# Buffer lifetimes that count transfers, and a re-ordered feed-forward schedule, in a one-core diffusion step

## Chip, cores and metric

The kernel runs on one core of one Trainium2 chip. The metric is the device time of one launch in microseconds (us), here the median of three runs. TensorE is called PE, VectorE DVE, ScalarE ACT, GpSimd POOL and SyncE SP, as in the profile.

## What is computed

One inference step of a hybrid diffusion backbone with two layers over 128 prompt tokens and 1024 sample tokens, model width 1024. Layer 0 mixes tokens with a gated long convolution (Hyena), layer 1 with differential attention; each is followed by a gated ConvFFN of hidden width 2816. Cut to what matters here, each layer is:

```python
hp = modulate(rmsnorm(xp, norm_w[i, 0]), mp[0], mp[1])       # xs in the same way, with ms
yp = hyena_mixer(hp, ...) if i % 2 == 0 else diff_attention(...) @ at_w_out[j]
xp = xp + mp[2] * rmsnorm(yp, norm_w[i, 1])
hp = modulate(rmsnorm(xp, norm_w[i, 2]), mp[3], mp[4])
xp = xp + mp[5] * rmsnorm(conv_ffn(hp, *ff), norm_w[i, 3])

def conv_ffn(h, w_up, w_dw, b_dw, w_down):
    u = dwconv3(h @ w_up, w_dw, b_dw)
    g, val = jnp.split(u, 2, axis=-1)
    return (jax.nn.silu(g) * val) @ w_down
```

The modulations `mp`, `ms` are `silu(cond) @ w_ada + b_ada`, six vectors of 1024 for each layer and each of the two conditions. All of it is float32.

## The kernel before

**Arithmetic.** A float32 operand is split into two parts of PE's format, `hi` and `lo` (`split`, L207), and a product is three matmuls: hi by hi, hi by lo, lo by hi. The split is made in one of two ways: ACT writes `hi` (L208) and DVE writes `lo = src - hi` (L213); or, with `dma=True`, ACT writes `hi` (L208) and `-hi` (L210), and POOL issues a transfer that adds the source onto it (L211, `lo<-s`, `lo<-wr` in the profile).

**Order of work.** The program is a generator-driven list of steps, written out by hand. Each engine runs its instructions in the order in which the program emits them, so an instruction that waits holds all behind it on its engine. The program runs first in a dry mode (`Dry`, L39): it counts operations on a clock and notes for every on-chip buffer when it was made and last used. `place` (L82) then gives each buffer an address in one arena, larger ones first, wanting first a distance of 1000 operations between the last use of what lay there and the new use, then less, down to 0; it tries fillings of the arena of 100%, 98% and so on down. A buffer that takes the place of another waits for the last instructions that used it. A buffer that a transfer reads or writes counts as free from the operation after the one that issued the transfer.

**The ConvFFN** (`ffn`, L634; it runs twice) takes nine tiles of 128 tokens in three columns of three tiles. Phase 1 loops over 22 groups `g` of 128 hidden channels for the first column: `up` for the gate and the value (24 matmuls each, lines L657 to L659), `conv` and `gate_val` on ACT and DVE, and `down0(g - 1)` (L680) into six of the eight PSUM banks, which stay pinned. Two banks rotate among everything else. After `down0` a queue of generators is advanced (`advance`, L603): first the norms of the tiles of the other columns, `prenorm_pair` (L481), whose two halves each transpose four blocks into a bank (L500) and evict it with four ACT instructions (L503, `hc`); then `combine` (L529), which builds the seven operands of a Strassen-like product. Phase 2 takes columns two and three together, in 22 steps `j` of seven products (`product`, L727, matmuls at L736, 12 each). Helpers lie along the products by the table `ALONG`: `total` sums weights on DVE (L709, tile `s`), `both` splits by the transfer (tile `lo`), `evac` takes results out of PSUM (L740 on DVE, L745 on ACT), `side` and `middle` convolve. The helpers of the steps before the first product (t from -19 to -1) are called at the ends of groups 19 to 21 in phase 1. After the first two products `down0(21)` and `tail(0)` follow: the post-norm (`postnorm`, L584) of the first column, for which `tail` loads three tiles `x` (L579).

**Modulations of the next layer** come from the generator `extra` over `ada_rows` (L346): each step issues on SP a load of 512 KB (`adaw`), and runs two 1024-wide DVE instructions (L372) on the tile loaded a step earlier. It is stepped once for each of nine tiles in the output projection ahead of the ConvFFN (the loop at L1983), after `down0` in groups below 13 of phase 1, and in odd steps of phase 2. One of its steps announces by its value (`busy`) that PE work follows in the next one; the queue isn't advanced in between. On the way it calls `ab_from` (L380), which loads a small vector (`abw`) and uses it at once on DVE.

The few lines that set the order around the change are in phase 1 of `main`:

```python
if g > 0:
    down0(g - 1)
if g > 1 and not busy:
    advance(queue, 2 if g < 9 else 1)
busy = next(extra, None) if g < 13 else None
split_w(g, 2)
if g == NJ - 1:
    advance(queue, -1)
for t in range(6 * (g - NJ), 6 * (g - NJ) + 6):
    if t >= -19:
        along(t)
```

## Time and profile before

| what | value |
|---|---|
| median of three runs | 3182.41 us (3173.52 to 3183.02) |
| profiled execution, its own time | 3175.89 us |
| span of the profile, first to last instruction | 3174.1 us |
| busy share of the span: PE, DVE, ACT, POOL | 97%, 67%, 54%, 20% |
| mean granted TensorE clock | 0.986 |
| DMA, mean over the span | 164 GB/s |

The span is the time from the first to the last instruction, and 1.8 us of the profiled execution lie around it. The waits of an engine are its idle times, each put down to the last instruction or transfer that released it. The granted clock is 1.00 at 2.4 GHz and 0.50 at 1.2 GHz; a window over a stretch gives its mean.

### The profile page before, as it was taken

The numbers are of one execution on the slowest core, as the hardware profiler recorded it, in microseconds if no ns is written. First come the engines' busy times: TensorE is split into PE (matmuls) and PEld (weight loads), VectorE is DVE, ScalarE is ACT, GpSimd is POOL, SyncE is SP. The second block draws the span as 40 slices with busy tenths as digits, with TensorE's granted clock in tenths as the row PEclk, the third lists the DMA queues.
The fourth block names the chain that finished last, engine by engine and source line by source line (L and its number), as shares of the span: only waits on it lengthen the run. The fifth ranks groups of instructions, "written<-read, shape, count | busy, mean of one in ns | idle before, by whom it ended". The sixth has DMA issues, their size and how long they took to land.

```text
span 3174.1 us, 46733 instructions
## 1 busy us (share of the span) xinstructions
PE 3063.5 (97%) x17332; PEld 2839.3 (89%) x17332; DVE 2136.7 (67%) x3057; ACT 1720.0 (54%) x3185; POOL 619.3 (20%) x1010
## 2 busy tenths in 40 slices
PE   8999999899998899999999999999999998999998
PEld 5999998678997899988899999999888998999987
DVE  5678887765775777775654447789465666767743
ACT  5444445444544566654533338899535445666632
POOL 3111111230001222301133422223220002222100
PEclk9999999999999999999999999999999999999999
DMA  6354455853435788786464464353453346888753
GB/s 250 91 138 124 110 135 145 220 201 138 164 115 163 171 197 196 161 303 237 174 197 154 136 190 112 98 140 104 147 204 128 108 139 156 189 181 189 228 203 123
DMA packets 190136, 520.48 MB, mean 164 GB/s; under 512 B 25730, under 2 KB 53986, under 8 KB 189908
## 3 DMA queue, kind: packets, MB, share of 16 engines
q1 hardware_dynamic: 137428, 394.94, 37.4%
q0 software_dynamic: 52480, 122.56, 19.1%
q8 instruction: 136, 2.23, 0.3%
q14 instruction: 92, 0.75, 0.1%
HBM read 354.50 MB, written 68.13 MB: 133 GB/s over the span
## 4 chain that ended last, share of the span: by engine, by line
PE 50%; issue 3%; DMA 3%; DVE 2%; ACT 2%; POOL 1%; POOLq 0%; DVEq 0%; ACTq 0%; SPq 0%
PE banks L680 14%; PE banks L736 8%; PE banks L1726 4%; PE banks L1757 4%; PE banks L1632 3%; PE banks L1633 3%; PE banks L1631 3%; PE banks L1938 2%; PE banks L1747 2%; PE banks L657 2%; PE banks L659 2%; PE banks L658 2%; DMA lo<-s 1%; DMA lo<-wr 1%; POOL lo L211 1%
## 5 line engine op out<-in xcount | busy, mean ns | idle before, releaser
L736 PE MATMUL banks<-pair,hi 128*128 128x386 f32 x2464 | 647.9, 344 | 30.3 <-DVE v L740 16.5
L736 PEld LDWEIGHTS banks<-pair,hi 128*128 128x128 f32 x2464 | 458.0, 192 | 37.6 <-DVE v L740 20.5
L213 DVE TENSOR_TENSOR lo<-wr,hi 128x1024 fp32r<-128x1024 f32 x247 | 304.5, 1233 | 202.6 <-ACT hi L208 196.4
L736 PE MATMUL banks<-pair,lo 128*128 128x386 f32 x1232 | 423.3, 344 | 8.0 <-DMA lo<-wr 8.0
L208 ACT ACTIVATE hi<-wr 128x1024 fp32r<-128x1024 f32 (+1 forms) x400 | 364.2, 911 | 110.2 <-DMA wr<-ffn_up 30.6
L211 POOL DMA_DIRECT2D lo<-wr x153 | 132.7, 867 | 862.3 <-ACT lo L210 620.9
L657 PE MATMUL banks<-hi,hi 128*128 128x388 f32 x704 | 242.5, 344 | 12.7 <-ACT hc L503 9.3
L680 PE MATMUL banks<-lo,hi 128*128 128x512 f32 x792 | 249.2, 394 | 2.1 <-DVE lo L213 2.1
L680 PE MATMUL banks<-hi,hi 128*128 128x512 f32 x792 | 249.8, 395 | 0.0
L659 PE MATMUL banks<-hi,lo 128*128 128x388 f32 x704 | 241.2, 343 | 8.7 <-DVE lo L213 8.7
L680 PE MATMUL banks<-hi,lo 128*128 128x512 f32 x792 | 248.8, 394 | 0.0
L736 PEld LDWEIGHTS banks<-pair,lo 128*128 128x128 f32 x1232 | 236.1, 192 | 9.0 <-DMA lo<-wr 8.9
L658 PE MATMUL banks<-lo,hi 128*128 128x388 f32 x704 | 241.2, 343 | 0.0
L210 ACT ACTIVATE lo<-hi 128x512 fp32r<-128x512 f32 (+1 forms) x265 | 187.0, 706 | 66.1 <-DMA lo<-s 28.9
L1731 DVE TENSOR_REDUCE mx<-banks 128x1 f32<-128x1152 f32 x128 | 173.4, 1355 | 69.2 <-PE banks L1726 62.5
L1325 PE MATMUL banks<-hi,hi 128*128 128x386 f32 (+1 forms) x576 | 200.1, 347 | 1.6 <-DVE hi L2056 1.0
L1631 PE MATMUL banks<-hi,hi 128*128 128x384 f32 (+1 forms) x576 | 199.4, 346 | 0.0
L1327 PE MATMUL banks<-hi,lo 128*128 128x386 f32 (+1 forms) x576 | 196.5, 341 | 2.0 <-DMA lo<-wr 1.9
L1632 PE MATMUL banks<-lo,hi 128*128 128x384 f32 (+1 forms) x576 | 196.7, 341 | 0.0
L1633 PE MATMUL banks<-hi,lo 128*128 128x384 f32 (+1 forms) x576 | 196.6, 341 | 0.0
L784 DVE SCALAR_TENSOR_TENSOR cv<-row,dw,cv 128x768 f32<-128x768 f32 x176 | 178.2, 1014 | 27.1 <-ACT cv L779 23.7
L1326 PE MATMUL banks<-lo,hi 128*128 128x386 f32 (+1 forms) x576 | 196.0, 340 | 0.0
(386 smaller groups left out, 6852.4 us busy)
## 6 DMA issues: line engine op xcount, KB each, us to landing
wr<-ffn_up SPq DMA_DIRECT2D x176, 512.0 KB
wr<-ffn_down SPq DMA_DIRECT2D x132, 512.0 KB
lo<-wr POOLq DMA_DIRECT2D x132, 256.0 KB, 3.7
adaw<-w_adat SPq DMA_DIRECT2D x56, 512.0 KB
lo<-s POOLq DMA_DIRECT2D x88, 256.0 KB, 4.1
x<-x_d SPq DMA_DIRECT2D x33, 512.0 KB
hid<-cv SPq DMA_DIRECT2D x44, 384.0 KB
hd<-hid SPq DMA_DIRECT2D x88, 192.0 KB
```

Of the source, the lines that this page charges most:

```text
L208: act.activation(hi, src, AF.Copy)
L213: dve.tensor_tensor(out=lo, in0=src, in1=f(hi), op=ALU.subtract)
L657: pe.matmul(pt[:, 0:n], wh[:, k, :], hh[:, k, 0:n], start=k == 0, stop=False)
L658: pe.matmul(pt[:, 0:n], wh[:, k, :], hl[:, k, 0:n], start=False, stop=False)
L659: pe.matmul(pt[:, 0:n], wl[:, k, :], hh[:, k, 0:n], start=False, stop=k == KT - 1)
L680: pe.matmul(accs[c][i][h], s_[:, o:o + P], w_[:, 512 * h:512 * h + 512], start=first and n == 0, stop=last and n == len(parts) - 1)
L736: pe.matmul(pt[:, 0:NP], w[:, k, :], t[:, k, :], start=q < 4 and k == 0 and i == 0, stop=k == 3 and i == 2, skip_group_check=q > 3)
L1325: pe.matmul(pt[:, 0:n], wh[:, k, :], hh[:, k, 0:n], start=k == 0, stop=False)
L1327: pe.matmul(pt[:, 0:n], wl[:, k, :], hh[:, k, 0:n], start=False, stop=k == KT - 1)
L1631: pe.matmul(pt[:, 0:m], wh[:, k, :], hh[:, k, b:b + m], start=k == 0, stop=False)
L1632: pe.matmul(pt[:, 0:m], wh[:, k, :], hl[:, k, b:b + m], start=False, stop=False)
L1633: pe.matmul(pt[:, 0:m], wl[:, k, :], hh[:, k, b:b + m], start=False, stop=k == KT - 1)
```

## The change

- `Dry` tells transfers from other operations. A buffer that a transfer used last counts as live for 40 operations longer; `place` tries this with the whole 40, then with three quarters, a half, a quarter and none of it, each time over all fillings. At the sizes of this program it settles with the whole 40 at a filling of 94%; the kernel before settles at 96%.
- The tile `hs2` moves from the fixed tiles into the arena, which grows by the same 4608 bytes.
- The helpers of the steps ahead of the first product are called in twos after each half of a group (`along2`) and not at its end; the final `advance(queue, -1)` comes after the last group.
- The queue is advanced once ahead of `down0` and once behind it, in all groups, where it was advanced twice behind it below group 9, and once from there on.
- The modulations step in all groups of phase 1, not in those below 13; in the output projection only for tiles below 6; and in phase 2 only in odd steps above 4.
- `tail(0)` no longer loads its three `x` tiles; each post-norm loads its own in its second step.
- A branch of `tail` that never applied is gone.

```diff
--- before.py
+++ after.py
@@ -20,7 +20,7 @@
 FF = 2816
 NJ = FF // P
 EPS = 1e-6
-ROOM = 205984
+ROOM = 210592
 NCOL = (388, 386, 386)
 NP = 386
 NOUT = (385, 384, 384)
@@ -44,10 +44,10 @@
             self.dry = dry
 
         def __getattr__(self, op):
-            return self.dry.note
+            return self.dry.transfer if op == "dma_start" else self.dry.note
 
     def __init__(self, nc):
-        self.nc, self.n, self.clock = nc, 0, 0
+        self.nc, self.n, self.clock, self.lag = nc, 0, 0, 0
         self.tensor = self.scalar = self.vector = self.gpsimd = self.sync = Dry.Engine(self)
         self.of, self.lives = {}, []
 
@@ -55,8 +55,14 @@
         for x in (*args, *kw.values()):
             i = self.of.get(x.tensor.name) if isinstance(x, bass.AP) else None
             if i is not None:
-                self.lives[i][2] = self.clock
+                self.lives[i][2:] = self.clock, self.lag
         self.clock += 1
+
+    def transfer(self, *args, **kw):
+
+        self.lag = 40
+        self.note(*args, **kw)
+        self.lag = 0
 
     def array(self, shape, dtype):
         self.n += 1
@@ -66,7 +72,7 @@
         t = self.array(shape, dtype)
         size = 4 * math.prod(shape[1:])
         self.of[t.tensor.name] = len(self.lives)
-        self.lives.append([-(-size // 32) * 32, self.clock, self.clock])
+        self.lives.append([-(-size // 32) * 32, self.clock, self.clock, 0])
         return t
 
     @contextmanager
@@ -81,11 +87,11 @@
 
 def place(lives, room):
 
-    size, first, last = np.array(lives, dtype=np.int64).T
-    n, end = len(lives), int(last.max()) + 2
+    size, first, until, lag = np.array(lives, dtype=np.int64).T
+    n, end = len(lives), int((until + lag).max()) + 2
     todo = np.lexsort((first, -size))
 
-    def attempt(fill):
+    def attempt(fill, last):
         spare = np.full(n, -1)
         for g in (1000, 600, 400, 250, 150, 100, 64, 32, 16, 8, 0):
             till = np.minimum(last + g, end - 2) + 1
@@ -112,10 +118,11 @@
             at[i], put[m], spare[i] = lo[free[0]], i, g
         return at.tolist()
 
-    for percent in range(100, 70, -2):
-        at = attempt(percent / 100)
-        if at is not None:
-            return at
+    for part in (4, 3, 2, 1, 0):
+        for percent in range(100, 70, -2):
+            at = attempt(percent / 100, until + lag * part // 4)
+            if at is not None:
+                return at
     raise MemoryError("the buffers do not fit")
 
 
@@ -592,6 +599,9 @@
             dve.scalar_tensor_tensor(out=junk[:, 512 * h:512 * h + 512], in0=acc[h], scalar=r,
                                      in1=gs[kind][:, 512 * h:512 * h + 512], op0=ALU.mult, op1=ALU.mult)
         yield
+        if x is None:
+            x = load_x(T)
+            yield
         dst, n = x_d[T] if out is None else out, 2 if T == NT - 1 else 1
         for h in range(n):
             r = slice(D // n * h, D // n * (h + 1))
@@ -802,6 +812,11 @@
                 if 0 <= j + d < NJ:
                     fn(*args, j + d)
 
+        def along2(ts):
+            for t in (next(ts), next(ts)):
+                if t >= -19:
+                    along(t)
+
 
         def load_down(m):
             if m < 2 * NJ:
@@ -824,7 +839,7 @@
             mm_down(c, parts, seq, js[0] == 0, js[-1] == NJ - 1)
 
         def tail(c):
-            posts, xs = [], [load_x(3 * c + i) for i in range(3)]
+            posts, xs = [], [load_x(3 * c + i) if c else None for i in range(3)]
             for i, x in enumerate(xs):
                 T = 3 * c + i
                 gen = postnorm(T, x, accs[c][i], gs, to_out(T) if nxt is None else None)
@@ -839,8 +854,6 @@
                 queue.extend(posts)
                 if late != ():
                     late.extend(nxt(3 * c + i, None) for i in range(3))
-                elif nxt is not None:
-                    queue.extend(nxt(3 * c + i, x) for i, x in enumerate(xs))
                 return
             pres = [] if nxt is None else [nxt(3 * c + i, x) for i, x in enumerate(xs)]
             for g in posts:
@@ -860,26 +873,28 @@
             queue.append(combine(hs))
             busy = None
             for g in range(NJ):
+                t = iter(range(6 * (g - NJ), 6 * (g - NJ) + 6))
                 load(g + 1, range(0 if g else 2, 3))
                 pg = up(g, 0)
                 cg = conv(g, 0, pg, NOUT[0])
                 split_w(g + 1, 0)
+                along2(t)
                 pv = up(g, 1)
                 cv = conv(g, 1, pv, NOUT[0])
                 split_w(g + 1, 1)
+                along2(t)
                 gate_val(cg, cv)
                 hid[g] = halves(cv, st, [NOUT[0]])
+                if g > 1:
+                    advance(queue, 1)
                 if g > 0:
                     down0(g - 1)
                 if g > 1 and not busy:
-                    advance(queue, 2 if g < 9 else 1)
-                busy = next(extra, None) if g < 13 else None
+                    advance(queue, 1)
+                busy = next(extra, None)
                 split_w(g, 2)
-                if g == NJ - 1:
-                    advance(queue, -1)
-                for t in range(6 * (g - NJ), 6 * (g - NJ) + 6):
-                    if t >= -19:
-                        along(t)
+                along2(t)
+            advance(queue, -1)
             for t in range(7 * NJ):
                 j, q = divmod(t, 7)
                 product(j, q)
@@ -889,7 +904,7 @@
                     tail(0)
                 elif q == 4:
                     advance(queue, 1)
-                elif q == 5 and j % 2:
+                elif q == 5 and j > 4 and j % 2:
                     next(extra, None)
                 if j == NJ - 1 and q < 5:
                     load_down(q)
@@ -1014,7 +1029,7 @@
         hvec = cst([P, 24, 5], F32, "hvec")
         nbin = cst([P, 24], F32, "nbin")
         fcol = cst([P, 4], F32, "fcol")
-        hs2 = cst([P, 9, P], F32R, "hs2")
+        hs2 = mem([P, 9, P], F32R, nm("hs2"))
         z2 = cst([P, 2], F32, "z2")
         yx_d = tc.dram_tile((NT, P, KT - 1, P), F32, name="yx_d")
 
@@ -1980,7 +1995,8 @@
                     if Tp < NT - 1:
                         next(pre[Tp])
                 post = (T, x)
-                next(extra, None)
+                if T < 6:
+                    next(extra, None)
             self.room = self.rest = None
             queue.extend(pre[T] for T in sorted(pre))
```

Where the program emits things then shows in three places.

**DVE at the end of the output projection, start of the first ConvFFN** (`x` is the last tiles' sum, `adaj` and `adaw` the modulations, `cv` the first convolutions, `lo` a weight's). Before:

```order
L592 SCALAR_TENSOR_TENSOR junk_6960<-banks,r_6967,G_6101 128x512 x2
L598 TENSOR_TENSOR x_6805<-x_6805,junk_6960 128x1024
L372 SCALAR_TENSOR_TENSOR adaj_6987,mcol_96<-adaw_6874,cb_6208 128x1024
L372 SCALAR_TENSOR_TENSOR adaw_6874,mcol_96<-adaw_6874,cb_6210 128x1024
L592 SCALAR_TENSOR_TENSOR junk_6990<-banks,r_6999,G_6101 128x512 x2
L598 TENSOR_TENSOR x_6906<-x_6906,junk_6990 128x512 x2
L372 SCALAR_TENSOR_TENSOR adaj_7009,mcol_96<-adaw_6985,cb_6208 128x1024
L372 SCALAR_TENSOR_TENSOR adaw_6985,mcol_96<-adaw_6985,cb_6210 128x1024
L376 TENSOR_TENSOR mcol_96<-mcol_96,bc_6214 128x16
L666 SCALAR_TENSOR_TENSOR cv_7040<-banks,dw,cv_7040 128x385
L667 SCALAR_TENSOR_TENSOR cv_7040<-banks,dw,cv_7040 128x385
L213 TENSOR_TENSOR lo_7048<-wr_6954,hi_7046 128x1024
```

With the change:

```order
L599 SCALAR_TENSOR_TENSOR junk_6974<-banks,r_6983,G_6127 128x512 x2
L608 TENSOR_TENSOR x_6818<-x_6818,junk_6974 128x1024
L599 SCALAR_TENSOR_TENSOR junk_7002<-banks,r_7011,G_6127 128x512 x2
L608 TENSOR_TENSOR x_6918<-x_6918,junk_7002 128x512 x2
L676 SCALAR_TENSOR_TENSOR cv_7048<-banks,dw,cv_7048 128x385
L677 SCALAR_TENSOR_TENSOR cv_7048<-banks,dw,cv_7048 128x385
L220 TENSOR_TENSOR lo_7056<-wr_6967,hi_7054 128x1024
L676 SCALAR_TENSOR_TENSOR cv_7084<-banks,dw,cv_7084 128x385
L677 SCALAR_TENSOR_TENSOR cv_7084<-banks,dw,cv_7084 128x385
```

The two pairs of modulations ahead of the first convolution are gone from here.

**ACT in group 21 of the first ConvFFN, up to the first products** (`hi<-wr` 128x512 and `hi<-s` are the products' operands, `cv` the group's convolutions, L665 and L675 the same instruction). Before:

```order
L665 ACTIVATE cv_9641<-banks,dw 128x385
L671 ACTIVATE cv_9612<-cv_9612 128x385
L208 ACTIVATE hi_9648<-cv_9641 128x385
L208 ACTIVATE hi_9671<-wr_9461 128x1024
L208 ACTIVATE hi_9676<-wr_9336 128x512
L210 ACTIVATE lo_9677<-hi_9676 128x512
L208 ACTIVATE hi_9692<-s_9584 128x512
L210 ACTIVATE lo_9693<-hi_9692 128x512
L719 ACTIVATE hi_9700<-s_9698 128x512
L208 ACTIVATE hi_9705<-s_9575 128x512
L210 ACTIVATE lo_9707<-hi_9705 128x512
L208 ACTIVATE hi_9714<-wr_9338 128x512
```

With the change:

```order
L675 ACTIVATE cv_9668<-banks,dw 128x385
L215 ACTIVATE hi_9674<-wr_9381 128x512
L217 ACTIVATE lo_9676<-hi_9674 128x512
L675 ACTIVATE cv_9715<-banks,dw 128x385
L215 ACTIVATE hi_9720<-s_9641 128x512
L217 ACTIVATE lo_9721<-hi_9720 128x512
L729 ACTIVATE hi_9729<-s_9726 128x512
L215 ACTIVATE hi_9732<-s_9555 128x512
L217 ACTIVATE lo_9733<-hi_9732 128x512
L681 ACTIVATE cv_9668<-cv_9668 128x385
L215 ACTIVATE hi_9741<-cv_9715 128x385
L215 ACTIVATE hi_9769<-wr_9508 128x1024
```

The operands of the first products now stand among the group's convolutions and ahead of its last `hi<-cv`, where they stood behind it.

**PE in group 2 of the first ConvFFN** (`xn` is the normed tile that is transposed; L680 and L690 are `down0`, L657 and L667 the next group's first matmul). Before:

```order
L680 MATMUL banks<-hi_7215,hi_7183 128x512 x2
L680 MATMUL banks<-lo_7216,hi_7183 128x512 x2
L680 MATMUL banks<-hi_7215,lo_7185 128x512 x2
L500 MATMUL banks<-ident,xn_6651 128x128 x4
L500 MATMUL banks<-ident,xn_6767 128x128 x4
L657 MATMUL banks<-hi_6348,hi_7258 128x388
```

With the change:

```order
L669 MATMUL banks<-hi_6372,lo_7188 128x388
L507 MATMUL banks<-ident,xn_6675 128x128 x4
L690 MATMUL banks<-hi_7224,hi_7194 128x512 x2
L690 MATMUL banks<-lo_7226,hi_7194 128x512 x2
L690 MATMUL banks<-hi_7224,lo_7195 128x512 x2
L690 MATMUL banks<-hi_7224,hi_7194 128x512 x2
L690 MATMUL banks<-lo_7226,hi_7194 128x512 x2
L690 MATMUL banks<-hi_7224,lo_7195 128x512 x2
L690 MATMUL banks<-hi_7224,hi_7194 128x512 x2
L690 MATMUL banks<-lo_7226,hi_7194 128x512 x2
L690 MATMUL banks<-hi_7224,lo_7195 128x512 x2
L507 MATMUL banks<-ident,xn_6675 128x128 x4
```

Four transposes go ahead of `down0` and four stay behind it, and both belong to one tile where they belonged to two.

## Rows read from the trace of the kernel before

**Rows 1.** The page, busy time of each engine with its share of the span and its instructions.

```profile
PE 3063.5 (97%) x17332; PEld 2839.3 (89%) x17332; DVE 2136.7 (67%) x3057; ACT 1720.0 (54%) x3185; POOL 619.3 (20%) x1010
```

**Rows 2.** Waits of PE: line waited for, us in total, times, longest us.

```profile
PE banks L736 <- DVE v L740: 16.5, 11, 5.7
PE banks L317 <- DMA lo<-adar: 10.4, 3, 5.4
PE banks L657 <- ACT hc L503: 9.3, 8, 1.2
PE banks L659 <- DVE lo L213: 8.7, 3, 4.6
PE banks L736 <- ACT u L745: 8.5, 3, 3.5
PE banks L736 <- DMA lo<-wr: 8.0, 3, 3.7
PE banks L657 <- ACT hi L208: 3.5, 2, 3.2
PE banks L736 <- DVE junk L592: 2.9, 2, 2.6
PE banks L736 <- ACT hi L208: 2.3, 2, 1.7
PE banks L680 <- DVE lo L213: 2.1, 1, 2.1
```

**Rows 3.** Windows over the stretches at the lower clock: busy per engine, PEclk, DMA share, GB/s.

```profile
994.40:1001.20 6.80, 5.08 (x16) 5.08 (x17) 1.90 (x3) 3.10 (x7) 1.33 (x3) 0.50 0.64 109
...
1018.30:1025.10 6.80, 5.75 (x18) 5.75 (x19) 3.29 (x5) 3.42 (x6) 1.08 (x2) 0.50 0.42 117
1042.20:1045.60 3.40, 3.40 (x13) 3.40 (x12) 2.00 (x3) 1.64 (x4) 0.85 (x1) 0.50 0.45 81
...
2352.90:2363.10 10.20, 6.71 (x21) 6.18 (x21) 8.49 (x14) 3.50 (x5) 0.00 (x0) 0.50 0.95 328
...
sum 78.30, PE 63.38 PEld 57.86 DVE 52.48 ACT 42.49 POOL 17.56; mean PE 4.88 PEld 4.45 DVE 4.04 ACT 3.27 POOL 1.35
```

**Rows 4.** Windows, a stretch of products at full clock.

```profile
2659.00:2669.00 10.00, 10.00 (x58) 10.00 (x57) 3.70 (x6) 4.47 (x8) 2.95 (x4) 1.00 0.78 175
```

**Rows 5.** Waits of DVE, same columns as PE's.

```profile
DVE s L709 <- DMA lo<-s: 82.0, 21, 6.1
```

**Rows 6.** The page, DMA issues: count, KB each, median us from issue to landing.

```profile
lo<-s POOLq DMA_DIRECT2D x88, 256.0 KB, 4.1
```

**Rows 7.** Timeline of DVE, start, us, instruction, idle before and releaser, first product loop.

```profile
1018.13 0.69 DVE L709 TENSOR_TENSOR s<-s,wr 128x512 f32<-128x512 f32 x1 [6.08 <-DMA lo<-s]
```

**Rows 8.** Timelines of ACT and of PE, group 2 of the first ConvFFN.

```profile
737.86 2.91 ACT L503 ACTIVATE hc<-banks,ab 128x128 f32<-128x128 f32 x8 [0.47 <-PE banks L500]
739.42 0.44 PE L657 MATMUL banks<-hi,hi 128*128 128x388 f32 x1 [1.16 <-ACT hc L503]
```

**Rows 9.** Timeline of DVE, start of the first ConvFFN.

```profile
704.71 1.22 DVE L372 SCALAR_TENSOR_TENSOR adaj<-adaw,cb 128x1024 f32<-128x1024 f32 x1
```

**Rows 10.** Timeline of POOL before the second ConvFFN.

```profile
2345.42 1.15 POOL L426 TENSOR_SCALAR v<-ss 128x1 f32<-128x1 f32 x1 [4.04 <-ACT xn L448]
...
2348.42 0.29 POOL L428 TENSOR_SCALAR v<-s,s 128x1 f32<-128x1 f32 x1
```

**Rows 11.** Timeline of DVE, end of the first product loop.

```profile
1364.49 0.24 DVE L387 SCALAR_TENSOR_TENSOR ab<-ab,abw 128x8 f32<-128x8 f32 x2 [4.64 <-DMA abw<-nwc]
```

**Rows 12.** Timeline of DVE, product loop of the second ConvFFN.

```profile
2773.01 0.69 DVE L709 TENSOR_TENSOR s<-wr,wr 128x512 f32<-128x512 f32 x1 [4.15 <-DMA lo<-s]
```

**Rows 13.** Timeline of ACT, group 19 to 20 of the first ConvFFN.

```profile
962.33 1.06 ACT L208 ACTIVATE hi<-wr 128x1024 fp32r<-128x1024 f32 x1 [6.83 <-DMA wr<-ffn_up]
```

**Rows 14.** Windows, one group of the first ConvFFN with its modulation step.

```profile
837.00:850.00 13.00, 13.00 (x70) 12.22 (x70) 11.20 (x15) 6.79 (x9) 0.00 (x0) 1.00 0.49 159
```

**Rows 15.** Timeline of DVE, a step of `combine` in that group.

```profile
849.51 1.76 DVE L540 TENSOR_TENSOR t<-hc,hc 128x1544 f32<-128x1544 f32 x1
```

## Prediction

> **What bounds the kernel now.** I read the page first: PE is busy 3063.5 of 3174.1 us [rows 1], so it is the bound, and the change neither removes nor adds a product. What it can give back is PE's idle time, some 110 us, and what PE loses where its granted clock is low. Then the waits of PE say whom it waits for [rows 2]: in the product loops for DVE and ACT (L740, L745: 16.5, 8.5 and 2.9 us), at the first products for operands (8.0 and 2.3), at the norms' evictions (9.3), at the starts of the ConvFFNs for weights' parts (8.7 and 3.5), in the prelude for `lo<-adar` (10.4). Next the windows over the stretches at the lower clock [rows 3]: 78.30 us at PEclk 0.50, with PE busy for 63.38. Each stretch begins at or just after one of those waits. In one, 18 matmuls take 5.75 us, 0.32 each; at full clock 58 take 10.00, 0.17 each [rows 4]. So some 0.45 of the busy time of such a stretch is lost, 28 us in all. A wait that goes takes its stretch with it, if the neighbouring waits go too.
>
> The waits of DVE show what stands behind the loop's waits: 82.0 us in 21 waits of `s` (L709) for transfers `lo<-s` [rows 5], which land 4.1 us after issue [rows 6]. The example to look at: DVE stands 6.08 us at L709 until a `lo<-s` lands at 1018.1 [rows 7], and behind it stands the `v` (L740) for which PE waits 5.7, the longest of that row [rows 2]. No data flow ties that sum to that transfer: its buffer lies where the transfer's source lay, and the planner counted the source as free when the transfer was issued.
>
> **The change, part by part.**
>
> *Lifetimes that last to the landing.* With 40 operations more, by an estimate 4 to 7 us at the loops' pace, the planner leaves none of the close reuses behind a transfer (some 120 before, counted from the addresses). Loop waits of PE: 16.5 + 8.5 + 2.9 = 27.9 [rows 2]. Their stretches: 5.75 and four of 3.40 like the one at 1042.2 [rows 3] (the others at 1059, 1097 and 2677), 19.35 x 0.45 = 8.7. Together 36.6; I leave 4 for waits for PE's own results and for late weight loads, and take 32 (ends 12 and 37). The lower end is what is left if only the waits of over 3 us go that name one transfer. In the prelude one buffer of `adar` waits for a transfer in the same way; but the three accumulates there follow one another on POOL's queue, and one keeps its whole 2.2. Of 10.4 I take 7 with a little clock (ends 0 and 13). `tail(0)`'s loads of `x`, which stood on SP ahead of the weights' loads until their buffers were free, go with this term.
>
> *First products.* PE's waits here are 8.0 + 2.3 = 10.3 over both ConvFFNs [rows 2], plus two stretches of some 5.08 busy [rows 3], 2 x 5.08 x 0.45 = 4.6. With the change ACT has the operands ready before the group's last `hi<-cv`, and each transfer has `down0` as its cover. In the first ConvFFN a modulation (2.45 us of DVE) now stands ahead of the last `lo` of `down0(21)`: 1.3 back, and 0.5 elsewhere. 14.9 - 1.8 = 13 (ends 8 and 15).
>
> *Norms.* Two banks' transposes stood together, and PE had to wait for four evictions, 1.16 us, eight times [rows 2, 8]. The eight evictions take 2.91 [rows 8], 0.36 each. Now `down0` (4.35 us) lies between the banks, and the first bank's evictions are hidden by it; the second's begin when `down0` ends, because ACT's `hi<-cv` waits for the same moment, and about one eviction of 0.35 plus 0.2 stays per group. 9.3 - 8 x 0.5 = 5.4 (ends 0 and 9.3).
>
> *Modulations.* At the starts of the ConvFFNs two pairs of L372 (2 x 1.22 us each [rows 9]) go from DVE's path, in which `x`, the first convolutions and the weight's `lo` follow. PE's waits there are 8.7 + 3.5 = 12.2, of which 0.9 lies elsewhere (at 963). The `lo` comes about 2.5 to 3 us earlier in each of the two; the norm chain and the two convolutions stay. 11.3 falls to 5.6, and with some clock (6.71 busy in the second's stretch [rows 3]) I take 6.5 (ends 2 and 16). `ab_from`, for which DVE stood 4.64 at the loop's end [rows 11], moves into a step where DVE has room: PE's 2.1 [rows 2] and 3.40 x 0.45 = 1.5 go, 0.7 comes back: 2.9 (ends 0 and 3.6).
>
> On POOL the norm's first step takes 1.15 us while an L372 runs, and its like 0.29 otherwise [rows 10]. The Trainium skill, SBUF — State Buffer, section "SBUF: two separate sides", calls the port pair that DVE and GpSimd share an exclusive lock which an operation with two SBUF inputs holds to its end. By that rule the nine more steps in phase 1 would speak against the change: POOL's work could come up to 2.45 us later beside each. The rows agree for the small step, but the issues of accumulates on POOL hardly vary (847 to 1080 ns over the run), so by the rule the sum would be lower by at most 2 x 2.45, by the trace by nothing.
>
> *New costs.* The fullest groups so far, with a modulation and one step of `combine`, have 11.20 us of DVE in 13 and PE waits for nothing there [rows 14]. Now two steps of `combine` (1.76 each [rows 15]) and a modulation meet in some of them: 12.96 of 13, and DVE's own waits on top. That is 0 to 3. Each step's load stands on SP behind a wait for its buffer and ahead of the next weights' loads; the place that shows the pattern is 962.3, where ACT waited 6.83 for `wr<-ffn_up` [rows 13] and PE lost 0.9. Six to eight such places instead of two or three: 0 to 8. I take 5 for both.
>
> **Sum.** 32 + 7 + 13 + 5.4 + 6.5 + 2.9 - 5 = 62. Against the profiled execution's 3175.9 that is 3114; the median of the runs is 6.5 higher, and I put half of that on top: 3117, 2% below. A measurement of this kernel can tell about 0.3% (9.5 us) from no change.
>
> **Rivals.**
>
> *The waits were hidden, or new ones take their place.* For: in the second ConvFFN's loop DVE stands 4.15 us for `lo<-s` [rows 12] every 15 us step, and PE there waits almost nothing; many of the 82.0 us are of that kind. Also the planner packs tighter to pay for the 40 operations, and reuses behind PE's reads of under 20 operations, by ACT, nearly double (37 to 70). Then the loops give 12 and the prelude 2, `down0`-covered parts remain: 12 + 2 + 10 + 4 + 5 + 1 - 5 = 29, 3147, with the runs' offset up to 3153. Against: the loop's waits of PE are each traced to such a reuse.
>
> *All of it goes, the clock too.* 37 + 13 + 15 + 9 + 16 + 3.6 = 93 less 10 for the norm chains at the starts: 83, 3093. [...] Against: at the starts PE has nothing else to run.
>
> *Slower: the modulations' loads hold the weights.* In groups 11 to 21 of the first ConvFFN the load of `adaw` has a buffer that lies over a `hi` of `down0`; SP waits until PE has read it, and the next group's two weight loads stand behind. If they come late by all of the 6.83 us that ACT waited at 962.3 [rows 13], each of the 11 groups loses about 7: 77, against 62 gained, 3190. It decides from 5.7 us per group on; below that it eats the gain. Against: at 963 PE lost 0.9 of those 6.83.
>
> *Nothing changes.* The parts gain and a few of these late loads, at 3 to 5.6 us each in a dozen groups, take it back: 3173 to 3190.
>
> **How the numbers follow.** Forecast (3100 to 3133) 0.60; waits hidden or replaced (3147) 0.17; all goes (3093) 0.13; nothing 0.05; slower 0.05. The range 3091 to 3153 holds the first three, 0.90 by the cases, some of which lie outside; its ends are the second case with the runs' offset and the third, less 2 for the runs' spread. Faster by over 0.3%: 0.60 + 0.17 + 0.13 = 0.90; same 0.05; slower 0.05.
>
> **What would show it.** In the profile after: DVE's waits of `s` for `lo<-s` fall from 82.0 to under 15; PE's loop waits from 27.9 to about 4; no wait of 3.7 at the first products; the waits for `hc` eight times about 0.4; at most three stretches at the lower clock in the two ConvFFNs. The forecast is wrong if those waits go and the span falls by less than 45 us, or if PE waits for `wr<-ffn_up` through ACT's `hi` in several groups of phase 1.

## The result, and the profile after

The changed kernel takes 3126.21 us (median of four, 3125.18 to 3127.04) against 3179.38 for the kernel before in the same session: a ratio of 0.983, 95% interval 0.982 to 0.985, 53 us faster. The forecast was 3117 with a range of 3091 to 3153, from a sum of 62 us. The profiled span fell from 3174.1 to 3124.9 us.

The page of the changed kernel, busy time of each engine:

```profile
PE 3044.9 (97%) x17332; PEld 2823.7 (90%) x17332; DVE 2143.6 (69%) x3057; ACT 1729.7 (55%) x3185; POOL 619.2 (20%) x1010
```

PE is still the bound, with 80 us of idle time where there were 110 [rows 1]; of the 49.2 us of span that went, 30.6 are idle time and 18.6 busy time of the same 17332 matmuls. Its waits in the changed kernel (line waited for, us in total, times, longest; the rows that bear on the argument); lines have moved: L736 is L746, L740 L750, L745 L755, L657 L667, L659 L669, L680 L690, L592 L599, L709 L719, L213 L220, L208 L215, L210 L217, L503 L510.

```profile
PE banks L746 <- DVE junk L599: 9.8, 2, 5.4
PE banks L667 <- ACT hc L510: 8.2, 10, 2.4
...
PE banks L690 <- DVE lo L220: 5.9, 6, 2.2
PE banks L1342 <- DMA lo<-wr: 5.7, 5, 3.0
PE banks L507 <- DVE cv L677: 2.9, 1, 2.9
...
PE banks L690 <- ACT hi L215: 2.3, 2, 1.5
PE banks L324 <- DMA lo<-adar: 2.1, 2, 1.4
...
PE banks L669 <- DVE lo L220: 1.8, 2, 1.2
...
PE banks L746 <- DMA lo<-wr: 0.7, 1, 0.7
...
PE banks L746 <- DVE v L750: 0.2, 1, 0.2
```

Set against [rows 2]: the loops' waits for L740 and L745 (16.5 and 8.5) are 0.2; the first products' waits for `lo<-wr` (8.0) 0.7; the waits for weights' parts (8.7 and 3.5) 1.8 and 0.3, of which 1.2 are at a ConvFFN's start; `adar` 2.1 for 10.4. But `junk` stands at 9.8 for 2.9, the transposes (L507) now wait, the `down` products wait 8.2 (L690) for 2.1, and in the stage ahead of the first ConvFFN PE waits 5.7 (L1342) for 1.9, 3.0 of it in one place at 385. DVE's waits of `s` for `lo<-s` are 3.2 for 82.0 [rows 5]:

```profile
DVE s L719 <- DMA lo<-s: 3.2, 2, 2.4
```

Windows over the stretches at the lower clock in the changed kernel (columns as in [rows 3]):

```profile
384.50:391.30 6.80, 5.97 (x18) 5.98 (x19) 6.66 (x9) 0.00 (x0) 0.00 (x0) 0.50 0.05 18
565.40:575.60 10.20, 7.63 (x18) 4.83 (x17) 10.03 (x19) 10.01 (x12) 4.13 (x5) 0.50 1.07 224
797.50:804.30 6.80, 4.10 (x13) 3.73 (x14) 3.12 (x6) 4.26 (x10) 0.00 (x0) 0.50 0.20 78
893.10:896.50 3.40, 3.40 (x10) 2.63 (x9) 1.21 (x2) 1.63 (x2) 0.00 (x0) 0.50 0.87 334
998.90:1002.30 3.40, 3.40 (x10) 2.64 (x9) 0.88 (x2) 1.02 (x2) 1.31 (x2) 0.50 0.73 126
1005.70:1012.50 6.80, 4.47 (x14) 4.47 (x15) 5.28 (x9) 3.90 (x12) 3.52 (x7) 0.50 0.40 71
2606.50:2613.30 6.80, 3.46 (x11) 3.47 (x12) 4.27 (x7) 4.91 (x15) 4.07 (x8) 0.50 0.52 149
sum 44.20, PE 32.44 PEld 27.75 DVE 31.44 ACT 25.73 POOL 13.03; mean PE 4.63 PEld 3.96 DVE 4.49 ACT 3.68 POOL 1.86
```

44.2 us where there were 78.3 [rows 3]; none lies in a product loop past its first step, and none at a ConvFFN's start. By stages, cut at the starts of the first and last matmul of each in the traces (us; the runs are described below):

| stage | before | change | lives_only | no_lag | lag_max | lag_lead | best30 |
|---|---|---|---|---|---|---|---|
| to the first ConvFFN | 696.1 | 689.6 | 686.4 | 698.0 | 683.0 | 689.8 | 688.7 |
| its phase 1 | 295.7 | 300.4 | 295.1 | 303.1 | 300.3 | 287.5 | 286.1 |
| its product loop | 370.3 | 343.5 | 341.5 | 389.3 | 335.7 | 343.2 | 337.2 |
| its other `down` groups | 193.7 | 191.2 | 194.1 | 190.9 | 191.2 | 190.6 | 190.8 |
| attention layer | 785.0 | 785.9 | 786.4 | 786.2 | 787.9 | 784.7 | 789.9 |
| second ConvFFN, phase 1 | 296.0 | 285.3 | 294.8 | 285.7 | 287.4 | 286.1 | 285.8 |
| its product loop | 346.6 | 338.3 | 341.8 | 348.1 | 334.6 | 337.3 | 333.5 |
| its other `down` groups | 181.1 | 181.6 | 179.7 | 179.7 | 182.3 | 181.3 | 182.5 |

The loops gave 35 us, the second ConvFFN's phase 1 10.7, the stretch to the first ConvFFN 6.5. The first ConvFFN's phase 1 grew by 4.7. The two phases do not have the same steps: SP issues 14 loads of modulations in the first's (8 before) and 3 in the second's. Two places in the ConvFFNs took time back.

**A load that waits holds the loads behind it.** SP's, ACT's and PE's timelines in the first ConvFFN (start, us, instruction, idle before and releaser):

```profile
773.28 14.13 SPq L414 DMA_DIRECT2D G<-m_d  x2
787.46 0.90 SPq L654 DMA_DIRECT2D wr<-ffn_up  x2
...
794.18 1.06 ACT L215 ACTIVATE hi<-wr 128x1024 fp32r<-128x1024 f32 x1 [7.42 <-DMA wr<-ffn_up]
795.14 0.66 ACT L675 ACTIVATE cv<-banks,dw 128x385 f32<-128x385 f32 x1
...
797.83 1.09 PE L507 MATMUL banks<-ident,xn 128*128 128x128 f32 x4 [2.93 <-DVE cv L677]
801.29 0.69 PE L667 MATMUL banks<-hi,hi 128*128 128x388 f32 x1 [2.38 <-ACT hc L510]
```

The second of two loads of `G` (the norm's gains, a step of `extra` that now falls into group 6) has a buffer in which the planner had put a tile `x` that POOL still read; SP stood on it until 787.4. The weights behind it reached ACT at 794.2; the convolution queued behind ACT's `hi` held its PSUM bank, and PE's transposes wanted that bank. 5.3 us, and the stretch at 797.5.

**The post-norm of the first column.** ACT and PE after the first products:

```profile
999.30 0.61 ACT L215 ACTIVATE hi<-wr 128x512 fp32r<-128x512 f32 x1
1003.45 0.63 ACT L217 ACTIVATE lo<-hi 128x512 fp32r<-128x512 f32 x1 [3.54 <-DMA lo<-wr]
...
1004.88 0.59 ACT L595 ACTIVATE junk<-banks 128x512 f32<-128x512 f32 x1
...
1008.03 1.01 PE L746 MATMUL banks<-pair,hi 128*128 128x386 f32 x2 [4.46 <-DVE junk L599]
```

PE needs one of the six pinned banks for its next product, and gets it when the post-norm's squares (L595) and DVE's scaling are done. The squares stand behind an L217 whose buffer is a weight tile that a transfer still reads. The change's 40 operations did not protect that tile: `note` overwrites the margin with that of the last use, and DVE sums the same tile (L719) after the transfer was issued. The margin went back to 0.

### The profile page after: what moved, and what is told of

Its sections match the earlier page's. It is cut to its first block, busy times and chain, and to the rows that moved or that the text cites. A ratio compares the mean times of both kernels' runs of the same rounds, so it can differ in the third digit from the quotient of the medians.

```text
span 3124.9 us, 46695 instructions
## 1 busy us (share of the span) xinstructions
PE 3044.9 (97%) x17332; PEld 2823.7 (90%) x17332; DVE 2143.6 (69%) x3057; ACT 1729.7 (55%) x3185; POOL 619.2 (20%) x1010
## 5 line engine op out<-in xcount | busy, mean ns | idle before, releaser
L746 PE MATMUL banks<-pair,hi 128*128 128x386 f32 x2464 | 639.1, 341 | 10.0 <-DVE junk L599 9.8
L746 PEld LDWEIGHTS banks<-pair,hi 128*128 128x128 f32 x2464 | 453.2, 190 | 11.4 <-DVE junk L599 10.7
L215 ACT ACTIVATE hi<-wr 128x1024 fp32r<-128x1024 f32 (+1 forms) x400 | 365.2, 913 | 150.4 <-DMA wr<-ffn_up 47.6
L220 DVE TENSOR_TENSOR lo<-wr,hi 128x1024 fp32r<-128x1024 f32 x247 | 305.4, 1237 | 204.8 <-ACT hi L215 203.4
L746 PE MATMUL banks<-pair,lo 128*128 128x386 f32 x1232 | 419.1, 340 | 0.7 <-DMA lo<-wr 0.7
L690 PE MATMUL banks<-lo,hi 128*128 128x512 f32 x792 | 250.2, 396 | 5.9 <-DVE lo L220 5.9
L690 PE MATMUL banks<-hi,hi 128*128 128x512 f32 x792 | 251.7, 398 | 2.3 <-ACT hi L215 2.3
L690 PE MATMUL banks<-hi,lo 128*128 128x512 f32 x792 | 249.9, 395 | 0.0
L667 PE MATMUL banks<-hi,hi 128*128 128x388 f32 x704 | 240.6, 342 | 8.5 <-ACT hc L510 8.2
L669 PE MATMUL banks<-hi,lo 128*128 128x388 f32 x704 | 239.1, 340 | 1.8 <-DVE lo L220 1.8
L746 PEld LDWEIGHTS banks<-pair,lo 128*128 128x128 f32 x1232 | 233.3, 189 | 1.0 <-DMA lo<-wr 1.0
L1342 PE MATMUL banks<-hi,lo 128*128 128x386 f32 (+1 forms) x576 | 197.1, 342 | 5.8 <-DMA lo<-wr 5.7
L217 ACT ACTIVATE lo<-hi 128x512 fp32r<-128x512 f32 (+1 forms) x265 | 187.0, 706 | 18.6 <-DMA lo<-wr 6.2
L690 PEld LDWEIGHTS banks<-lo,hi 128*128 128x128 f32 x792 | 148.8, 189 | 43.2 <-DVE lo L220 9.3
```

Source lines behind the costliest of these rows:

```text
L215: act.activation(hi, src, AF.Copy)
L220: dve.tensor_tensor(out=lo, in0=src, in1=f(hi), op=ALU.subtract)
L667: pe.matmul(pt[:, 0:n], wh[:, k, :], hh[:, k, 0:n], start=k == 0, stop=False)
L669: pe.matmul(pt[:, 0:n], wl[:, k, :], hh[:, k, 0:n], start=False, stop=k == KT - 1)
L690: pe.matmul(accs[c][i][h], s_[:, o:o + P], w_[:, 512 * h:512 * h + 512], start=first and n == 0, stop=last and n == len(parts) - 1)
L746: pe.matmul(pt[:, 0:NP], w[:, k, :], t[:, k, :], start=q < 4 and k == 0 and i == 0, stop=k == 3 and i == 2, skip_group_check=q > 3)
```

## Experiments

Eleven runs, each timed against the kernel before on the same chip. The runs came in three sessions on three chips, and the change was timed in another; the kernel before took 3175.2, 3182.0, 3176.6 and 3179.4 us there. So a difference in us between runs of two sessions is good to some 4 to 7 us, and the ratios to before are the better comparison: by them lag_max is some 9 us ahead of the change, and first_back and mods_back some 9 behind it.

| run | us | ratio to before, interval |
|---|---|---|
| lives_only | 3131.1 | 0.986, 0.985 to 0.988 |
| no_lag | 3194.0 | 1.006, 1.004 to 1.007 |
| lag_max | 3113.4 | 0.981, 0.979 to 0.982 |
| lag_lead | 3111.1 | 0.980, 0.978 to 0.982 |
| norms_back | 3123.4 | 0.982, 0.980 to 0.984 |
| first_back | 3136.5 | 0.986, 0.985 to 0.988 |
| mods_back | 3137.1 | 0.986, 0.985 to 0.988 |
| best30 | 3105.7 | 0.976, 0.975 to 0.978 |
| best30_again | 3108.0 | 0.979, 0.976 to 0.981 |
| best20 | 3108.2 | 0.978, 0.975 to 0.981 |
| best30_60 | 3104.7 | 0.978, 0.975 to 0.980 |

### lives_only: the planner alone

The kernel before with the change's `Dry`, `place`, `ROOM` and `hs2`.

> The kernel before with nothing changed but the planner (40 operations more behind a transfer, hs2 in the arena); order of all steps as before. If the loops' waits went because of where buffers lie, then PE's waits for L740 and L745 in the product loops fall from 25.0 us to under 4 here too, the first ConvFFN's loop with its clock gives some 25 us and the second's some 8, and the time is about 3144 us (3135 to 3155). The waits at the first products (8.0 for lo<-wr) and the eight for hc (9.3) stay. If instead the re-ordering took the waits away (fewer modulations in the loop, the x loads put off), they stay above 15 us and the time is above 3165 us.

PE's waits in the loops are 1.4 and 1.3 us, and the time is 44 us under before, 13 below the 3144 expected: where buffers lie was the cause, and the longer lifetimes alone give most of the change (with `hs2` in the arena, which no run tries by itself). The first products' waits stay, those for `hc` too:

```profile
PE banks L664 <- ACT hc L510: 9.3, 8, 1.2
...
PE banks L743 <- DMA lo<-wr: 7.5, 2, 3.8
...
PE banks L743 <- ACT u L752: 1.4, 1, 1.4
PE banks L743 <- DVE v L747: 1.3, 2, 0.7
```

### no_lag: the re-ordering alone

```diff
-        self.lag = 40
+        self.lag = 0
```

> The changed kernel with 0 in place of 40 operations: all re-ordering, no longer lifetimes. If addresses are the cause, DVE waits again for lo<-s for 50 us and more, PE's waits in the loops (L750, L755) come back with 15 to 28 us and their clock, and the time is 3150 to 3170 us. If the re-ordering is the cause, it is within 10 us of 3126 us.

19 us slower than before, worse than either theory said. DVE waits 76.1 us for `lo<-s` again, and the re-ordered program meets longer ones; the worst, DVE's and PE's timelines:

```profile
1145.87 1.22 DVE L379 SCALAR_TENSOR_TENSOR adaj<-adaw,cb 128x1024 f32<-128x1024 f32 x1 [12.10 <-DMA lo<-wr]
...
1154.74 1.01 PE L746 MATMUL banks<-pair,hi 128*128 128x386 f32 x2 [10.62 <-ACT u L755]
```

A modulation whose buffer a transfer still used stood 12.1 us on DVE, and PE 10.6 behind it. The first product loop alone is 19.0 us longer than before (389.3 for 370.3). So the parts do not add: the re-ordering costs 19 us with the old lifetimes and gives 5 to 9 with the new (3131.1 to 3126.2, by the medians or by the ratios); the lifetimes give 44 on the old order and some 70 on the new. Each of these is one placement of the buffers; how much another placement of the same order would move them was not tried.

### lag_max: the margin kept through later uses

```diff
-                self.lives[i][2:] = self.clock, self.lag
+                self.lives[i][2:] = self.clock, max(self.lag, sum(self.lives[i][2:]) - self.clock)
```

> The changed kernel, but the 40 operations behind a transfer are kept when another operation uses the buffer after the transfer was issued (in the change that later use sets them back to 0: a weight tile that a transfer still reads is handed on because DVE summed it last). Theory: that is why ACT waited 3.5 us ahead of the post-norm of the first column; PE's 9.8 us for DVE junk (4.5 and 5.4, one in each ConvFFN) fall under 2, their stretches at the lower clock go too, 10 to 14 us in all: 3112 to 3117 us. Rival: PE waits there for the post-norm's own chain of ACT, POOL and DVE, which nothing hides now that the first products are ready: the 9.8 stay above 7 and the time stays within 4 us of 3126, but for what other buffers' new places do (5 us either way).

13 us faster than the change by the medians, and ACT's wait ahead of the squares is gone. That the number came out as forecast is in part luck: the two loops gave 11.5 us, the stretch ahead of the first ConvFFN, where this post-norm has no part, gave 6.6, and the other stages took some 5 back. PE's wait for `junk` is 4.4 and not under 2, so the rival holds for that part: six ACT instructions still stand in front of the squares.

```profile
PE banks L746 <- DVE junk L599: 4.4, 2, 2.5
```

### lag_lead: and loads that find their buffers free

```diff
+                if self.lag and i not in self.used:
+                    self.lives[i][1] = max(0, self.clock - 40)
+                self.used.add(i)
```

> lag_max, and a buffer that a transfer writes first counts as live from 40 operations before that transfer is issued, so that SP finds it free. Theory: the new waits in phase 1 of the first ConvFFN (2.9 and 2.4 us at 798 and 801, 3.3 at 876 to 892, 0.9 at 910) come from weight loads that SP issues late, since a load in front of them waits for its buffer; then ACT's wait for wr<-ffn_up falls from 47.6 to under 10 us, those PE waits and two stretches at the lower clock go, and it is another 8 to 14 us faster than lag_max: 3100 to 3108 us. Rival: the waits are DVE's (two steps of combine and a modulation in a group of 13 us) and the loads would have been covered: within 4 us of lag_max, the waits for L220 and L215 at 876 to 892 stay.

ACT's wait for `wr<-ffn_up`, 47.6 us in the change and 27.7 in lag_max, fell to 8.3, and phase 1 from 300.3 to 287.5, with the second ConvFFN's at 286.1: the late loads cost 13 us there. The time is only 2 us under lag_max, inside the noise: two stages grew, by 6.8 us ahead of the first ConvFFN, where PE's waits for `lo<-adar` are 8.8 for 1.5, and by 7.5 in its loop (a wait of 2.6 for ACT's `u` among them). That the planner's tighter places are the cause is likely and was not tried.

### norms_back: two banks' transposes together again

```diff
-                if g > 1:
-                    advance(queue, 1)
                 if g > 0:
                     down0(g - 1)
-                if g > 1 and not busy:
-                    advance(queue, 1)
+                if g > 1:
+                    advance(queue, 1 if busy else 2)
```

> The changed kernel, but the queue is advanced twice behind down0 (once where a modulation asks for a pause) and not once on either side: the same steps, two banks' transposes together again. The prediction's term: one bank at a time is worth 2.7 us per ConvFFN. Then the waits for hc (L510) are 1.2 us each again, and the first rows after them show it; 4 to 7 us slower than the change, about 3131 us, if nothing else moves. Rival: the halves on either side of down0 are what lets a late weight load stop PE at the transposes (2.9 and 2.4 us at 798 in the change); then those 5 us go and the time is within 3 us of 3126. Buffers' new places can add 5 us either way.

No difference from the change that the intervals can tell. The 1.16 us waits are back in both ConvFFNs (9.7 us for `hc`), and the second's phase 1 is 3.8 us longer. In the first's it is the same 300.4: the late load now stops PE at the next group's first matmul (4.2 us for `cv`), so the rival falls. The 3 us that the stretch ahead of the first ConvFFN is shorter, where this step has no part, is buffers' places.

### first_back: the first operands at the end of the groups again

```diff
                 split_w(g, 2)
-                along2(t)
-            advance(queue, -1)
+                if g == NJ - 1:
+                    advance(queue, -1)
+                for _ in range(3):
+                    along2(t)
```

with the two other calls of `along2` removed.

> The changed kernel, but the helpers of the steps ahead of the first product are called at the ends of groups 19 to 21 again, and the queue is emptied ahead of them. Theory from the profile after: the 3.7 us waits for lo<-wr at the first products come back in both ConvFFNs, but the post-norm's wait (9.8 us for DVE junk) falls to about 3, since PE comes later while the same ACT work is done: the term's 13 us were mostly handed on to the next wait, and the time is 3125 to 3132 us. Rival (the prediction's term): 13 us slower, 3139 us, with the junk wait where it is.

10 us slower than the change by the medians, between the two theories. In the second ConvFFN the term is worth nothing: the 3.75 us for `lo<-wr` come back, the post-norm's 5.4 fall to 0.2, and phase 1 and loop are 624.0 us against 623.6. In the first they are 8.5 us longer, since the transfer that PE waits for landed late. POOL's and PE's timelines:

```profile
989.62 0.96 POOL L218 DMA_DIRECT2D lo<-wr  x1 [204.70 <-ACT lo L217]
...
999.36 0.69 PE L746 MATMUL banks<-pair,lo 128*128 128x386 f32 x1 [10.03 <-DMA lo<-wr]
```

and the window over it (busy per engine, PEclk, DMA share, GB/s):

```profile
989.00:1000.00 11.00, 0.97 (x4) 0.65 (x4) 5.52 (x8) 5.55 (x10) 4.37 (x5) 0.53 0.96 246
```

The accumulate issued at 989.6 let PE go at 999.4. SP issued four loads of 512 KB between 987.9 and 990.2, and the 16 DMA engines were busy for 0.96 of that window.

### mods_back: the modulations where they were

```diff
-                busy = next(extra, None)
+                busy = next(extra, None) if g < 13 else None
-                elif q == 5 and j > 4 and j % 2:
+                elif q == 5 and j % 2:
-                if T < 6:
-                    next(extra, None)
+                next(extra, None)
```

> The changed kernel with the modulations' steps where they were (nine in the output projection, groups below 13, all odd steps of phase 2). By the prediction's term it is 9 us slower less the 5 of new costs, and PE's waits at the starts of the ConvFFNs come back (4.5 us and 6.6 with their clock in the kernel with the lifetimes alone): in the second ConvFFN about 9 us. Against that the first ConvFFN's phase 1 loses its late weight loads and the waits of down0 in groups 13 to 21, and is 5 to 8 us shorter than the change's 300.4. So 3124 to 3134 us; under 3120 says that the move cost more than it gave.

11 us slower by the medians, 3 above the range expected. The second ConvFFN's phase 1 is 296.7 for 285.3, with PE's waits of 3.2 and 3.7 at its start back; `ab_from` costs 2.8 again in the `down` groups (195.4 for 191.2); the first's phase 1 is 4.0 shorter, not 5 to 8.

### best30 and its neighbours

lag_max with 30 operations of lead, no modulation in group 21, and the post-norm ahead of step 1's helpers:

```diff
                 product(j, q)
-                along(t)
                 if t == 1:
                     down0(NJ - 1)
                     tail(0)
-                elif q == 4:
+                along(t)
+                if q == 4:
```

> A version that takes up what the runs showed: lag_max, 30 operations of lead for buffers that a load writes first, no modulation in group 21 (it stands ahead of the lo that down0(21) waits for, 1.3 to 2.2 us), and down0(21) with the first column's post-norm emitted ahead of the helpers of step 1, so that its squares stand in front on ACT. If PE's wait at the post-norm is ACT's order, it falls from 2.5 and 1.9 us (lag_max) under 1.2 each; phase 1 of the first ConvFFN is as in lag_lead (287.5 us), the loop as in lag_max (335.7): 3095 to 3105 us. If the tighter places give new waits elsewhere, 3105 to 3115 us.

> best30 once more, for a closer interval: 3103 to 3108 us, 2.3 to 2.5% under the kernel before.

> best30 with 20 operations of lead in place of 30. A load of weights is then issued later by a third; if 20 operations cover it, as the time from a load's issue to its use says, phase 1 stays at 286 us and the time is within 6 us of 3106 us, up or down by where buffers fall (in best30 the first column's squares wait 3.0 us for a buffer that down0(21) still reads, in the second ConvFFN they don't). If not, ACT's wait for wr<-ffn_up rises above 20 us and phase 1 of the first ConvFFN to 292 us or more.

> best30 with 60 operations behind a transfer in place of 40. The 45 reuses at 40 to 60 operations behind a transfer go; those behind PE's and DVE's reads under 20 operations grow from 142 to 178. If 40 operations are too short for transfers that land late, the product loops lose 1 to 3 us more and the time is 3100 to 3105 us; if 40 is enough, the closer reuses behind PE cost 2 to 8 us: 3107 to 3113 us.

best30 beats both kernels: 2.2 to 2.4% under before by its two medians, and 18 to 20 us under the change. Phase 1 is as expected (286.1), the loop 1.5 us longer than lag_max's, the time at the upper end of what was expected or just above. In the second ConvFFN PE's wait for `junk` falls from 1.9 in lag_max to 0.2, so there it was ACT's order; but PE now waits 0.9 and 0.6 there for `v` and `u`, so little of it is gained. In the first it still waits 3.2, and ACT's two timelines show why:

```profile
983.86 0.60 ACT L598 ACTIVATE junk<-banks 128x512 f32<-128x512 f32 x1 [2.95 <-PE banks L693]
...
2584.22 0.60 ACT L598 ACTIVATE junk<-banks 128x512 f32<-128x512 f32 x1 [0.27 <-PE banks L693]
```

The square could start when the first tile's banks are done, as at 2584; at 983 its `junk` lies over an operand that the whole of `down0` reads. The neighbours are within their intervals of it. With 20 operations of lead ACT waits 3.2 us for `wr<-ffn_up` and phase 1 is 287.3, so 20 cover the loads. In best30_60 neither expectation is borne out: the time is that of the first, but the two loops are not shorter (669.7 us for 669.7 in best30_again). DVE's waits for `lo<-s` are 0.9 us there, in best30_again 17.3, at the same time: waits of that kind that PE does not share are free, as the first rival said of the second loop [rows 12].

## Why the prediction was right, and where its steps were off

*Lifetimes, 32 and 7.* Right. The two loops fell by 33.6 us with the planner alone, the stretch ahead of the first ConvFFN by 9.7. In the full change that stretch fell by 6.5 only: `adar` gave 8.3, but a `lo<-wr` that landed late holds PE for 3.0 at 385, with the stretch at 384.5. The premise that none of the close reuses behind a transfer is left was wrong: a source that DVE sums after the transfer was issued lost its 40 operations, and lag_max shows what that cost. The rival of hidden waits falls for the waits that the term counted, but it is right about the rest of the 82 us.

*First products, 13.* The waits of 10.3 went to 0.7, but PE got 7 us more of `junk` and two stretches at the lower clock there. The step that failed is "each transfer has `down0` as its cover. ... 1.3 back": I asked what hides the new operands, not who is late once they are ready. That is ACT's order, and in best30 the place of `junk`, by 2 to 5 us; and the modulation ahead of the last `lo` cost 2.2 and not 1.3. Undone alone the step is worth some 8.5 us in the first ConvFFN and nothing in the second.

*Norms, 5.4.* Right in kind: nine waits of 0.64 us on average (8.2 less the one of 2.4; 0.5 was expected), worth 3.8 us in the second ConvFFN's phase 1 and not to be told from 0 over the kernel.

*Modulations, 6.5 and 2.9.* Too small. The starts' waits fell from 11.3 to 1.2, not 5.6, and their stretches at the lower clock went: 11.4 us in the second ConvFFN alone. With the modulations gone from in front of it the `lo` came in time; the norm chain that I kept as a floor was covered. `ab_from`'s stage gave 2.5 against the kernel before and 4.2 against mods_back, for 2.9.

*New costs, 5.* Too small, and the other half of the miss. Of "0 to 8" for late loads the first ConvFFN's phase 1 paid 13 (300.4 to 287.5 with free buffers). The mechanism of the rival that ends slower was real; its place was another (a load of `G` in group 6, over a tile that POOL read), and it held for one long stall and some short ones, not for eleven groups.

*The clock.* "Each stretch begins at or just after one of those waits" is not so for two of the thirteen stretches of [rows 3], 17.1 of the 78.3 us: those at 567.7 and 1567.8 stand behind waits that the list leaves out, and one of 6.8 us at 48.9 is not counted. No term used them. Nor did a stretch always go with its wait: where the first products had one of 6.8 us (994.4) the change has 3.4 at 998.9 and 6.8 at 1005.7, and the one of 13.7 at 567.7 is one of 10.2 at 565.4.

*The signs.* `lo<-s`, the loops' waits and the first products came as said. The waits for `hc` were nine of some 0.64 and one of 2.4, and not eight of 0.4, and five stretches at the lower clock lie in the two ConvFFNs where at most three were allowed. A sign of being wrong came too, PE held by late `wr<-ffn_up`: once for 5.3 us, in a few groups for less. The rival in which nothing changes had its price wrong: a dozen late loads at 3 us take back 36 and not 62.

*The sum* was 62; the medians differ by 53. The modulations gave more than their term, the first products gave less, and the new costs were larger, which nearly cancelled: that the total came within 9 us is in part luck, while the largest term, the lifetimes, was right by itself. What the prediction did not see at all is that the parts need each other: the re-ordering alone is 19 us slower than the kernel before. No run tries the later loads of `x` alone.

## What to carry to other kernels

When a planner reuses buffers by program order, give it both ends of a transfer: a buffer stays taken until the transfer has landed, whatever uses it in between, and one that a load fills must be free when the load reaches its queue, not when its data are wanted. When a wait is removed, name the next event on the same chain, here the release of a bank behind ACT's queue, and price that one before booking the gain. Measure parts of a change both alone and left out: here one part was worth 44 us alone and some 70 in company.

## What had not been expected of the hardware

In first_back a 256 KB accumulate issued on POOL's queue in the middle of four loads of 512 KB on SP's released PE 9.7 us later (989.6 to 999.4; DMA share 0.96 in that window), where the page's medians are 3.8 and 3.9 us. It is no single case. Of the accumulates `lo<-wr` and `lo<-s` in the trace of the change, the 201 with no load of 512 KB issued on SP in the 3 us before them landed 3.8 us after their issue in the median, the 28 with one such load 5.5, the 11 with two 6.6; in all thirteen traces the medians are 3.7, 5.8, 7.0 and, with three, 7.8. So a margin of 40 operations, 4 to 7 us by the prediction's estimate, does not always last to the landing. That the loads are the cause was not tried by itself.
